# Top-2 gate dispatch on one core: the early two-row store becomes a 64 KB store of zeros, and the first 16 rows are stored whole

## The chip, the cores and the metric

The kernel runs on one core of a Trainium2 chip. The time is the device time of one execution in microseconds (us), and the figure compared is the median of several executions. One core has a vector engine (DVE), a scalar engine (ACT), a general engine (POOL), a tensor engine (PE, not used here) and a synchronisation engine (SP). Sixteen DMA engines move data between the chip's main memory (HBM) and the on-chip memory of 128 partitions. A DMA is issued by one of the engines' instruction queues, written SPq or ACTq in the profile. The DMA transfers issued from SP appear there as queue q1, those from ACT as queue q10.

## What is computed

There are 16 x 1024 = 16,384 tokens. Each has a row x of 512 float32 numbers and 8 router logits. The reference takes a softmax over the 8 logits, keeps the two largest probabilities, smaller one first, scales them so that they sum to one, and writes the row of x twice, once multiplied by each weight:

```python
logits_max = np.max(router_logits, axis=-1, keepdims=True)
probs = np.exp(router_logits - logits_max)
probs = probs / np.sum(probs, axis=-1, keepdims=True)
topk_indices = np.argsort(probs, axis=-1)[..., -k:]          # k = 2
topk_probs = np.take_along_axis(probs, topk_indices, axis=-1)
topk_probs = topk_probs / np.sum(topk_probs, axis=-1, keepdims=True)
x_expanded = x[:, :, np.newaxis, :].repeat(k, axis=2)
return (x_expanded * topk_probs[..., np.newaxis]).astype(np.float32)
```

The inputs are 33.55 MB of x and 0.52 MB of logits; the output is 67.11 MB.

## The kernel before

The 16,384 tokens are laid over 128 partitions, 128 consecutive tokens ("rows") to a partition. So partition p owns 256 KB of x and 512 KB of the output, each in one contiguous piece of HBM. All 128 partitions always move together; "16 rows" below means 16 rows of every partition, 4 MB of x and 8 MB of output.

The **weights** come first. L72 loads all logits with one DMA. `top2_weights` (L26 to L42) finds the largest and second largest logit of every row by a small tournament of maxima and minima on DVE, takes their difference, and ACT turns it into the two weights `WA` by a sigmoid of the difference with each sign (L41, L42).

The **rows** then go in two groups of 64. A group has one input tile `xs` (64 rows a partition) and one extra output tile `osp` (16 rows of doubled output). In each group SP issues four loads of 16 rows (L96), and then DVE walks a plan of seven pieces (L83 to L91). For each piece one DVE multiplication (L99) reads n rows of `xs`, each twice, multiplies them by the two weights and writes 2n rows of output, and one DMA (L107) stores these. A doubled piece needs twice the space of its input, so the output is written over rows of `xs` that are already used up: rows 0 to 15 go to `osp`; rows 16 to 31 go to `low`, the space of rows 0 to 31 of `xs`; rows 32 to 47 go in two halves to `osp` again, after the first 16 rows have been stored from it; rows 48 to 63 go in two halves to `high`, the space of rows 32 to 63.

Two of the seven pieces belong to the first 16 rows: a piece of `e` = 2 rows and one of the other 14. In the first group alone (`rows.start == 0`, L106) the 2-row store is issued from ACT; every other store and every load is issued from SP.

Four things set the order around the change. SP issues strictly in program order: the logits, the four loads of a group, then this group's stores, each of which waits for its multiplication; then the four loads of the next group, which wait until the stores have left `xs`. DVE is in order too, and its third piece of a group (rows 32 to 39) waits until `osp` has been stored. DMAs of one queue are worked off in the order of issue on each of the 16 DMA engines. A DMA of the other queue is interleaved with these. Waits are put in by the framework from the reads and writes of the tiles. At the program's end SP waits for all DMAs (L138).

Of the kernel before, what the change touches and what calls it, by code (L numbers as in the profile page):

```python
# [1 line left out]

# [4 lines left out]

F32 = mybir.dt.float32
ALU = mybir.AluOpType
ACTF = mybir.ActivationFunctionType  # L10
P = 128


def top2_weights(nc, pool, logits, M, E):

    hi, lo, n = None, None, E
    while n > 1:  # L20
        n //= 2
        if hi is None:
            a, b = logits[:, :, 0:n], logits[:, :, n : 2 * n]
            nhi = pool.tile([P, M, n], F32, tag=f"hi{n}")
            nlo = pool.tile([P, M, n], F32, tag=f"lo{n}")
            nc.vector.tensor_tensor(nhi, a, b, op=ALU.max)  # L26
            nc.vector.tensor_tensor(nlo, a, b, op=ALU.min)  # L27
        else:
            a, b = hi[:, :, 0:n], hi[:, :, n : 2 * n]
            nhi = pool.tile([P, M, n], F32, tag=f"hi{n}")  # L30
            nlo = pool.tile([P, M, n], F32, tag=f"lo{n}")
            tmp = pool.tile([P, M, n], F32, tag=f"tmp{n}")
            nc.vector.tensor_tensor(tmp, lo[:, :, 0:n], lo[:, :, n : 2 * n], op=ALU.max)  # L33
            nc.vector.tensor_tensor(nlo, a, b, op=ALU.min)  # L34
            nc.vector.tensor_tensor(nlo, nlo, tmp, op=ALU.max)  # L35
            nc.vector.tensor_tensor(nhi, a, b, op=ALU.max)  # L36
        hi, lo = nhi, nlo
    dlt = pool.tile([P, M], F32, tag="dlt")
    nc.vector.tensor_tensor(dlt, hi[:, :, 0], lo[:, :, 0], op=ALU.subtract)  # L39
    WA = pool.tile([P, M, 2], F32, tag="WA")  # L40
    nc.scalar.activation(WA[:, :, 0], dlt, ACTF.Sigmoid, scale=-1.0)  # L41
    nc.scalar.activation(WA[:, :, 1], dlt, ACTF.Sigmoid, scale=1.0)  # L42
    return WA


@with_exitstack
def kernel(
    ctx: ExitStack,
    tc: tile.TileContext,
    x: bass.AP,  # L50
    router_logits: bass.AP,
    k: bass.AP,
    out: bass.AP,
):
    nc = tc.nc
    B, S, D = x.shape
    E = router_logits.shape[-1]
    N = B * S
    assert int(k) == 2 and E == 8 and N % P == 0
    M = N // P  # L60

    GROUP = 64
    L = 16
    x_v = x.rearrange("b s d -> (b s) d").rearrange("(p m) d -> p m d", p=P)
    o_v = out.rearrange("b s k d -> (b s) k d").rearrange("(p m) k d -> p m k d", p=P)
    rl_v = router_logits.rearrange("b s e -> (b s) e").rearrange(
        "(p m) e -> p m e", p=P
    )

    wpool = ctx.enter_context(tc.tile_pool(name="wpool", bufs=1))  # L70
    logits = wpool.tile([P, M, E], F32)
    nc.sync.dma_start(logits, rl_v)  # L72
    WA = top2_weights(nc, wpool, logits, M, E)

    xs = wpool.tile([P, GROUP, D], F32)
    osp = wpool.tile([P, L, 2, D], F32)


    low = xs[:, : 2 * L, :].rearrange("p (r k) d -> p r k d", k=2)
    high = xs[:, 2 * L :, :].rearrange("p (r k) d -> p r k d", k=2)  # L80
    h = L // 2
    e = 2
    plan = [  # L83
        (0, e, osp[:, :e]),
        (e, L - e, osp[:, e:]),
        (L, L, low),
        (2 * L, h, osp[:, :h]),
        (2 * L + h, h, osp[:, h:]),
        (3 * L, h, high[:, :h]),
        (3 * L + h, h, high[:, h:]),  # L90
    ]  # L91

    for g in range(M // GROUP):
        m0 = g * GROUP
        for r in range(0, GROUP, L):
            nc.sync.dma_start(xs[:, r : r + L, :], x_v[:, m0 + r : m0 + r + L, :])  # L96
        for r, n, og in plan:
            rows = slice(m0 + r, m0 + r + n)
            nc.vector.tensor_tensor(  # L99
                og,  # L100
                xs[:, r : r + n, :].unsqueeze(2).to_broadcast([P, n, 2, D]),
                WA[:, rows, :].unsqueeze(3).to_broadcast([P, n, 2, D]),
                op=ALU.mult,
            )

            queue = nc.scalar if rows.start == 0 else nc.sync  # L106
            queue.dma_start(o_v[:, rows], og)  # L107


# [1 line left out]
_INS = ['x', 'router_logits', 'k']  # L111
_OUTS = [((16, 1024, 2, 512), 'float32')]

_NUMBERS = {'k': 2}


# [26 lines left out]
```

## Time and profile before

| what | value | where it is read |
|---|---|---|
| median of five runs | 241.71 us (241.33 to 241.91) | the times |
| the profiled execution's own time | 241.76 us | the times |
| its span, first to last instruction | 240.0 us | page, first line |
| time outside the span | 1.8 us | difference of the two above |
| DVE busy | 142.1 us (59%) | page, part 1 |
| bytes moved by DMA | 101.19 MB, mean 422 GB/s | page, part 3 |
| one multiplication, 2 / 14 / 16 rows | 2.292 / 15.083 / 17.224 us | groups by form |
| issue of one DMA on SP / ACT | about 0.33 us / 0.376 us | tiles `out_dram`, `osp` |
| 2-row store from ACT: issue, issue to landing | at 16.64 us, 17.3 us | timeline, DMA issues |
| 2-row store from SP (second group): issue, issue to landing | at 134.39 us, 29.8 us | timeline, DMA issues |

The span is cut by the profile into 40 slices of 6 us; for each it gives the busy share of an engine in tenths. Beside this, stretches of any length can be asked for; such a row gives the busy time of each engine, the mean busy share of the 16 DMA engines and the GB/s that they moved. A packet is counted in the stretch in which it starts, so the share of a short stretch can exceed 1. Rate divided by share is then the speed of the DMA engines while they work, free of this effect.

### The profile page before, as it was taken

To read this page: it belongs to the slowest core of one execution; us is meant where nothing else is said; L and a number is where in the kernel's file an instruction comes from. 1 tells how busy PE (TensorE), PEld (TensorE's weight loads), DVE (VectorE), ACT (ScalarE), POOL (GpSimd) and SP (SyncE) were. 2 spreads that over 40 slices of the span, in tenths; PEclk is the share of its full clock that TensorE was granted. 3 is DMA by queue.
4 is the path that set the end of the run, shared out by engine and by line. 5 is a ranking of instruction groups with operands and counts; after the bars stand their busy time and mean duration, and the time that the engine had idled before them with its cause. 6 is when DMAs were issued, how large, how long until landed. Compare 5 with 4: busy or idle time off the path is not lost.

```text
span 240.0 us, 116 instructions
## 1 busy us (share of the span) xinstructions
DVE 142.1 (59%) x25; ACT 1.8 (1%) x3; POOL 0.2 (0%) x4
## 2 busy tenths in 40 slices
DVE  2369999910499999300000999997008999990000
ACT  2000000000000000000000000000000000000000
POOL 0000000000000000000000000000000000000000
DMA  7999999979989899999989999999989898999996
GB/s 262 437 437 389 459 419 426 526 335 440 503 350 524 350 437 437 437 437 437 437 350 437 437 437 437 437 355 531 421 376 503 371 502 355 431 437 437 437 437 262
DMA packets 3312, 101.19 MB, mean 422 GB/s; under 512 B 368, under 2 KB 368, under 8 KB 496
## 3 DMA queue, kind: packets, MB, share of 16 engines
q1 hardware_dynamic: 3168, 100.14, 97.7%
q10 hardware_dynamic: 144, 1.05, 1.0%
HBM read 34.08 MB, written 67.11 MB: 422 GB/s over the span
## 4 chain that ended last, share of the span: by engine, by line
DMA 49%; DVE 32%; issue 7%; SPq 1%; DVEq 0%
DMA out_dram<-osp 26%; DMA xs<-in_x_dram 23%; DVE osp L99 18%; DVE xs L99 15%; SPq L96 0%; SPq L72 0%; SPq L107 0%; DVEq L99 0%
## 5 line engine op out<-in xcount | busy, mean ns | idle before, releaser
L99 DVE TENSOR_TENSOR osp<-xs,WA 128x8192 f32<-128x8192 f32 (+2 forms) x8 | 69.2, 8688 | 69.0 <-DMA xs<-in_x_dram 40.0
L99 DVE TENSOR_TENSOR xs<-xs,WA 128x8192 f32<-128x8192 f32 (+1 forms) x6 | 69.2, 11536 | 0.2
L26 DVE TENSOR_TENSOR nhi<-logits 128x512 f32<-128x512 f32 x1 | 0.7, 691 | 4.5 <-DMA logits<-in_router_logits_dram 4.5
L41 ACT ACT_TABLE_LOAD x1 | 1.3, 1283 | 0.7 <-PEq L124 0.7
L33 DVE TENSOR_TENSOR tmp<-nlo 128x256 f32<-128x256 f32 (+1 forms) x2 | 0.7, 352 | 0.0
L34 DVE TENSOR_TENSOR nlo<-nhi 128x256 f32<-128x256 f32 (+1 forms) x2 | 0.7, 352 | 0.0
L36 DVE TENSOR_TENSOR nhi<-nhi 128x256 f32<-128x256 f32 (+1 forms) x2 | 0.7, 352 | 0.0
L35 DVE TENSOR_TENSOR nlo<-nlo,tmp 128x256 f32<-128x256 f32 (+1 forms) x2 | 0.7, 352 | 0.0
L27 DVE TENSOR_TENSOR nlo<-logits 128x512 f32<-128x512 f32 x1 | 0.7, 684 | 0.0
L41 ACT ACTIVATE WA<-dlt 128x128 f32<-128x128 f32 x1 | 0.3, 314 | 6.3 <-DVE dlt L39 6.3
L39 DVE TENSOR_TENSOR dlt<-nhi,nlo 128x128 f32<-128x128 f32 x1 | 0.3, 292 | 0.0
L42 ACT ACTIVATE WA<-dlt 128x128 f32<-128x128 f32 x1 | 0.3, 298 | 0.0
L124 POOL MEMSET const-bfloat16-1.0<- 128x1 bf16 x1 | 0.1, 101 | 0.0
L124 POOL MEMSET const-uint8-127<- 128x1 uint8 x1 | 0.1, 101 | 0.0
L124 POOL MEMSET const-float32-0.0<- 128x1 f32 x1 | 0.1, 98 | 0.2 <-issue 0.2
L124 POOL MEMSET const-float32-1.0<- 128x1 f32 x1 | 0.1, 98 | 0.0
## 6 DMA issues: line engine op xcount, KB each, us to landing
xs<-in_x_dram SPq DMA_DIRECT2D x8, 4096.0 KB, 36.8
out_dram<-osp SPq DMA_DIRECT2D x4, 4096.0 KB, 20.7
out_dram<-xs SPq DMA_DIRECT2D x4, 4096.0 KB, 22.7
out_dram<-osp SPq DMA_DIRECT2D x2, 7168.0 KB, 31.6
out_dram<-osp ACTq DMA_DIRECT2D x1, 1024.0 KB, 17.3
out_dram<-osp SPq DMA_DIRECT2D x1, 1024.0 KB, 29.8
logits<-in_router_logits_dram SPq DMA_DIRECT2D x1, 512.0 KB, 3.8
out_dram<-xs SPq DMA_DIRECT2D x2, 33.7
```

Of the source, the lines that this page charges most:

```text
L26: nc.vector.tensor_tensor(nhi, a, b, op=ALU.max)
L27: nc.vector.tensor_tensor(nlo, a, b, op=ALU.min)
L33: nc.vector.tensor_tensor(tmp, lo[:, :, 0:n], lo[:, :, n : 2 * n], op=ALU.max)
L34: nc.vector.tensor_tensor(nlo, a, b, op=ALU.min)
L35: nc.vector.tensor_tensor(nlo, nlo, tmp, op=ALU.max)
L36: nc.vector.tensor_tensor(nhi, a, b, op=ALU.max)
L39: nc.vector.tensor_tensor(dlt, hi[:, :, 0], lo[:, :, 0], op=ALU.subtract)
L41: nc.scalar.activation(WA[:, :, 0], dlt, ACTF.Sigmoid, scale=-1.0)
L42: nc.scalar.activation(WA[:, :, 1], dlt, ACTF.Sigmoid, scale=1.0)
L99: nc.vector.tensor_tensor(og, xs[:, r : r + n, :].unsqueeze(2).to_broadcast([P, n, 2, D]), WA[:, rows, :].unsqueeze(3).to_broadcast([P, n, ...
L124: nc = _bacc.Bacc("TRN2", target_bir_lowering=False, num_devices=1)
```

## The change

A tile `blank` of 128 partitions x 128 float32 (64 KB) is set to zero by DVE, and ACT stores it to a scratch tensor `spare` in HBM. Both instructions stand ahead of everything else in the program. The piece of 2 rows and the piece of 14 rows become one piece of 16, in both groups, and all stores of the output are issued from SP.

```diff
     wpool = ctx.enter_context(tc.tile_pool(name="wpool", bufs=1))
+    dpool = ctx.enter_context(
+        tc.tile_pool(name="dpool", bufs=1, space=bass.MemoryType.DRAM)
+    )
+
+
+    blank = wpool.tile([P, 128], F32)
+    spare = dpool.tile([P, 128], F32)
+    nc.vector.memset(blank, 0.0)
+    nc.scalar.dma_start(spare, blank)
+
     logits = wpool.tile([P, M, E], F32)
     nc.sync.dma_start(logits, rl_v)
     WA = top2_weights(nc, wpool, logits, M, E)
...
     h = L // 2
-    e = 2
     plan = [
-        (0, e, osp[:, :e]),
-        (e, L - e, osp[:, e:]),
+        (0, L, osp),
         (L, L, low),
         (2 * L, h, osp[:, :h]),
...
                 op=ALU.mult,
             )
-
-            queue = nc.scalar if rows.start == 0 else nc.sync
-            queue.dma_start(o_v[:, rows], og)
+            nc.sync.dma_start(o_v[:, rows], og)
```

## The prediction

> **What bounds the kernel.** I read the page's busy shares first, then the queue's own waits, then stretches around each change of direction between loads and stores. The page:
>
> ```profile
> span 240.0 us, 116 instructions
> DVE 142.1 (59%) x25; ACT 1.8 (1%) x3; POOL 0.2 (0%) x4
> ...
> DVE  2369999910499999300000999997008999990000
> ...
> DMA  7999999979989899999989999999989898999996
> ...
> HBM read 34.08 MB, written 67.11 MB: 422 GB/s over the span
> ```
>
> DVE has stretches of zeros; the DMA row has none. The chain of waits names DVE for 32% of the span, but while DVE works the DMA engines are full too, so its chain is not what sets the end: the bytes are. 101.19 MB in 240.0 us is 422 GB/s. What DVE and SP wait for costs nothing as long as the DMA engines keep a backlog. The timeline shows how much:
>
> ```profile
> 0.72 0.37 SPq L72 DMA_DIRECT2D logits<-in_router_logits_dram  x1
> 1.15 2.01 SPq L96 DMA_DIRECT2D xs<-in_x_dram  x4
> ...
> 14.31 17.29 DVE L99 TENSOR_TENSOR osp<-xs,WA 128x2048 f32<-128x2048 f32 x2 [6.00 <-DMA xs<-in_x_dram]
> 16.64 0.38 ACTq L107 DMA_DIRECT2D out_dram<-osp  x1
> 31.64 0.35 SPq L107 DMA_DIRECT2D out_dram<-osp  x1
> ```
>
> Four loads and the logits are 17.3 MB; at 433 GB/s (next view) that is 40.0 us from about 1.7 us, so to 41.7 us with nothing else. The 14-row store is queued at 31.64 us, 10 us earlier. The end has a margin too: the last multiplication ends at 215.9 us, the DMA engines work to about 239 us.
>
> So the time changes only if the engines move more bytes, stand idle, or work more slowly. For the last I asked for stretches (length; busy us of DVE, ACT and POOL with counts; clock; DMA share; GB/s):
>
> ```profile
> 18.00:24.00 6.00, 6.00 (x1) 0.00 (x0) 0.00 (x0) 1.00 1.01 389
> 24.00:33.00 9.00, 8.96 (x2) 0.00 (x0) 0.00 (x0) 1.00 1.02 440
> 44.00:46.00 2.00, 2.00 (x1) 0.00 (x0) 0.00 (x0) 1.00 1.68 721
> 118.00:125.00 7.00, 0.00 (x0) 0.00 (x0) 0.00 (x0) 1.00 1.03 393
> 125.00:157.00 32.00, 24.90 (x3) 0.00 (x0) 0.00 (x0) 1.00 1.01 437
> 157.00:160.30 3.30, 3.30 (x1) 0.00 (x0) 0.00 (x0) 1.00 0.95 328
> ```
>
> Rate over share is the engines' speed: 437/1.01 = 433 GB/s in the undisturbed stretch. Time lost in a stretch is share x length less bytes/433. 18 to 24 us: 6.06 - 389 x 6/433 (5.39) = **0.67 us**; this is where the ACT store's packets come among the loads. 118 to 125 us, stores to loads: 7.21 - 6.35 = 0.86. 157 to 160.3 us, loads to stores: 3.14 - 2.50 = **0.64 us**. 44 to 46 us, also loads to stores: 3.36 - 3.33 = **0.03 us**. I have no name for the cause, but four places and their sizes stand in the trace, and the change touches three.
>
> **The change, part by part.**
>
> *Merged multiplications.* In each group 2.292 + 15.083 us become the 16-row form, 17.224 us in its own row. The pair takes 17.29 us in the timeline, so 0.07 us is saved on DVE, worth nothing under the backlog. One L107 issue (0.33 us on SP, in the second group at 134.39) and the ACT issue go; nothing waits for either.
>
> *Whole store, same bytes.* In each group a 1 MB and a 7.3 MB store become one of 8.4 MB. The small packets' own price: 24 to 33 us, where they are interleaved, runs at 440/1.02 = 431, undisturbed 433; 0.4% of 9 us is 0.03 us, twice: **-0.06 us**. The whole store is issued at about 31.6 us, 10 us before the loads are through; should this cover go, each late microsecond costs one. `osp` comes free when it has landed: 17.3 + 0.07 + 8.4 MB = 25.8 MB, the same bytes as before plus 64 KB, so DVE's third piece still starts near 63.3 us, and its store at 72 us stands before the 16-row store behind it has drained (8.4 MB, 19.4 us, to about 81). Cover 9 us. In the second group the store was due at 149.4 us and the loads last to 160: cover 11 us.
>
> *Memset and wait.* The memset is not in the trace. From below by POOL's 128x1 memset (0.098 us), from above by DVE's 128x128 subtraction (0.292 us); I take 0.2. DVE is idle until 4.54 us, so 0. ACT waits for it before issuing; behind that wait stand the table load (1.28 us) and the sigmoids, due at 8.35 us. Some 0.6 us late, the load ends near 2.6: 5.7 us to spare, 0. SP does not wait.
>
> *The scratch store.* Issued near 1 us and 0.38 us long, its first packets come near 2 us, among those of the logits: ahead of the big loads, not of the logits, whose issue begins at 0.72. Everything in the DMA backlog behind it moves. Logits late by 0.9 us would still give weights at 9.8 us, against rows at 14.2. Its price on the engines, lower end: 65.5 KB at 433 GB/s, **0.15 us**. Upper end: the Trainium skill, "DMA: Bandwidth & Descriptors", section Bandwidth, calls transfers under 64 KB dominated by descriptors and measures 0.95 us for 64 KB alone, loaded by another issuing path. By bytes the whole sum is 0.67 us lower than I get below, by the page's figure 0.13 us higher. The nearest row decides: the only other first store of ACT's queue cost 0.67 us of speed at 18 to 24 us. I take 0.15 + 0.67 = **+0.82 us**. No row lets the store bring time directly, and a gain could come only through the stretches below.
>
> *What was paid for the old early store* goes with it: **-0.67 us**.
>
> *First group, loads to stores near 42 us.* Before, 0.03 us, eleven microseconds after the early store's packets. Now nothing has been written to the output by then and no store has run for 38 us. The second group before is the nearest row: pure loads for 37 us, then stores, 0.64 us. From below 0 more (the scratch store readies whatever the early store readied), from above +0.61 by this row, and more if a first touch of the output is dearer. I choose the row: **+0.61 us**. At 118 us nothing changes. At 157 us the first store becomes the whole one; I keep the 0.64, since the one first store of that size in the trace (14 rows, 44 us) is cheap in a place that differs in more than size (second rival).
>
> Sum: 0.82 - 0.67 + 0.61 - 0.06 = **+0.70 us**. The profiled span goes from 240.0 to 240.7 us, its time from 241.76 to 242.46; from the median, 241.71 + 0.70 = **242.4 us** (0.29% slower).
>
> **Rivals.**
>
> *The scratch store does the early store's work.* Then the first-store price only moves from 18 us to 2 us and 42 us stays at 0.03: 0.82 - 0.67 - 0.06 = +0.09, **241.8 us**. The same time comes out if the scratch store costs its bytes alone and only the price at 42 us is new: 0.15 - 0.67 + 0.61 - 0.06 = +0.03. For it: 0.03 us at 44 us against 0.64 at 157. Against: the 64 KB are over near 3 us, and go elsewhere in HBM.
>
> *The 8 KB-a-partition stores are what slows the engines.* This is the other side. Both load-to-store stretches with a loss have the 2-row store as their first store; the one without has the 14-row store. If size decides, both losses end: -0.67 - 0.64 - 0.06 + 0.15 = -1.22, **240.5 us**; with +0.82 for the new small store, -0.55, **241.2 us**. It decides if 42 and 157 us both show some 0.03. Against it: 118 us loses 0.86 us with packets of one size (32 KB) on both sides.
>
> *A first write with no loads beside it is dear.* The ACT store's first packets came late, and loads filled that time. Bare at 42 us, its whole latency would show: issue at 16.64, signs of it from 18 to 24, so up to 2 us beyond my sum: **244.4 us**. Against: loads had no such price at their start.
>
> *The change does not do what it says*: the scratch store might come after the first loads of x. By the issue times it cannot be far behind, and its price is the same there; no separate case.
>
> **How the numbers follow.** Forecast 0.46, first rival 0.26, second 0.21, third 0.07. A measurement of this kernel tells about 0.2%, 0.48 us, from no change. The forecast's spread is 0.4 us either way, so some of it falls under that bound, some of the first rival above it. Slower: 0.36 + 0.07 + 0.07 = 0.50. Same: 0.10 + 0.17 + 0.02 = 0.29. Faster: 0.02 + 0.19 = 0.21. The forecast alone spans 242.0 to 242.8. For 8 in 10 the low end is 240.4, just under all of the second rival; the high end 243.4 leaves out most of the third.
>
> **What would show it.** Right: a stretch near 2 us with a loss near 0.8 us, none at 18 to 24 us, a loss near 0.6 us at 41 to 45 us, and 118 and 157 us as before. If 42 us shows 0.03, the first rival holds; if 157 us also shows none, the second. Any DMA slice below 9 between 31 and 81 us, other than by counting, would mean that a cover I relied on has gone, and the whole sum with it.

## The result and the profile after

The changed kernel takes **242.11 us** (median of 28 runs, 241.72 to 242.76); the kernel before took 241.72 us in 48 runs beside it (241.33 to 242.47). The ratio is **1.0017**, 95% interval 1.0012 to 1.0022: slower by 0.39 us by the medians, 0.29 to 0.53 us by the interval. That is a slowdown clear of zero, though 0.17% is less than the 0.2% (0.48 us) that the prediction counted as just visible.

The page of the changed kernel, with the rows that answer to those of before. Of the last row: the scratch store, its bytes and the time from issue to landing.

```profile
span 240.4 us, 115 instructions
...
DMA  7999999898989899999989999999999998999995
...
HBM read 34.08 MB, written 67.17 MB: 421 GB/s over the span
...
spare<-blank ACTq DMA_DIRECT2D x1, 64.0 KB, 3.7
```

The DMA row still has no gap: its eights stand beside nines, as before, because a packet counts in the slice in which it starts. No stretch of idle DMA engines was opened; the 0.4 us of span must come from bytes or from speed. Now the order of the work, from the timeline of the changed kernel:

```profile
0.73 0.38 SPq L82 DMA_DIRECT2D logits<-in_router_logits_dram  x1
0.82 0.17 DVE L78 MEMSET blank<- 128x128 f32 x1 [0.82 <-PEq L130]
1.02 0.34 ACTq L79 DMA_DIRECT2D spare<-blank  x1
1.16 2.08 SPq L104 DMA_DIRECT2D xs<-in_x_dram  x4
1.39 1.28 ACT L41 ACT_TABLE_LOAD   x1 [1.39 <-DVE blank L78]
...
14.52 17.22 DVE L107 TENSOR_TENSOR osp<-xs,WA 128x16384 f32<-128x16384 f32 x1 [6.19 <-DMA xs<-in_x_dram]
31.77 0.35 SPq L113 DMA_DIRECT2D out_dram<-osp  x1
...
63.65 17.29 DVE L107 TENSOR_TENSOR osp<-xs,WA 128x8192 f32<-128x8192 f32 x2 [14.65 <-DMA out_dram<-osp]
```

The third piece in the kernel before:

```profile
63.30 17.29 DVE L99 TENSOR_TENSOR osp<-xs,WA 128x8192 f32<-128x8192 f32 x2 [14.43 <-DMA out_dram<-osp]
```

The scratch store is issued at 1.02 us, between the logits and the first load of x. The first multiplication starts at 14.52 us (before: 14.31), the third piece at 63.65 (before: 63.30). So 0.21 us of delay is there before the first multiplication, and it grew to 0.35 by 64 us. Three stretches of the DMA engines say where (the last two numbers of a row are DMA share and GB/s). The kernel before, then the changed one:

```profile
18.00:24.00 6.00, 6.00 (x1) 0.00 (x0) 0.00 (x0) 1.00 1.01 389
38.00:47.00 9.00, 9.00 (x1) 0.00 (x0) 0.00 (x0) 1.00 1.05 451
156.00:162.00 6.00, 6.00 (x1) 0.00 (x0) 0.00 (x0) 1.00 0.94 355
```

```profile
18.00:24.00 6.00, 6.00 (x1) 0.00 (x0) 0.00 (x0) 1.00 1.01 437
38.00:47.00 9.00, 9.00 (x1) 0.00 (x0) 0.00 (x0) 1.00 1.10 441
156.00:162.00 6.00, 6.00 (x1) 0.00 (x0) 0.00 (x0) 1.00 1.16 437
```

By the prediction's sum (share x length less bytes/433, good to about 0.07 us in 9 us because the share has two digits) the loss at 18 to 24 us went from 0.67 to 0.00 us. At 38 to 47 us it went from 0.08 to 0.73: that is where the loads run out and the stores begin. At 156 to 162 us, the same switch in the second group, it was 0.72 and is 0.90. One loss vanished and one of about the same size appeared 22 us later, as forecast. Over 18 to 47 us this pair of profiles leaves nothing to explain +0.39 us. Single profiles scatter, so the same stretches were measured in twelve more kernels.

One thing can be read already: which packets are slow. The 38 to 47 us of the changed kernel, cut at 43.1 us (by the packet records of the trace, the first 64 KB packet, which only the whole store has, starts at 43.19 us):

```profile
40.00:43.10 3.10, 3.10 (x1) 0.00 (x0) 0.00 (x0) 1.00 1.01 338
43.10:47.00 3.90, 3.90 (x1) 0.00 (x0) 0.00 (x0) 1.00 1.24 538
```

0.71 us are lost in the first row and none in the second. The last loads before the stores are slow; the packets of the stores run at the undisturbed speed. So it is at the early store of the kernel before: its first packet starts at 20.94 us, and 0.30 of the 0.67 us are lost before it:

```profile
18.00:20.90 2.90, 2.90 (x1) 0.00 (x0) 0.00 (x0) 1.00 0.94 362
```

### The profile page after: what moved, and what is told of

Same layout as the page of the kernel before. It is cut to its first block, busy times and chain, and to the rows that moved or that the text cites. A ratio compares the mean times of both kernels' runs of the same rounds, so it can differ in the third digit from the quotient of the medians.

```text
span 240.4 us, 115 instructions
## 1 busy us (share of the span) xinstructions
DVE 142.1 (59%) x24; ACT 1.8 (1%) x3; POOL 0.2 (0%) x4
## 4 chain that ended last, share of the span: by engine, by line
DMA 46%; DVE 36%; issue 7%; SPq 0%; DVEq 0%
DMA out_dram<-osp 27%; DVE osp L107 22%; DMA xs<-in_x_dram 19%; DVE xs L107 14%; SPq L82 0%; SPq L113 0%; DVEq L107 0%
## 5 line engine op out<-in xcount | busy, mean ns | idle before, releaser
L107 DVE TENSOR_TENSOR osp<-xs,WA 128x8192 f32<-128x8192 f32 (+1 forms) x6 | 69.0, 11534 | 69.4 <-DMA xs<-in_x_dram 39.9
```

What stands on the lines that cost most here:

```text
L107: nc.vector.tensor_tensor(og, xs[:, r : r + n, :].unsqueeze(2).to_broadcast([P, n, 2, D]), WA[:, rows, :].unsqueeze(3).to_broadcast([P, n, ...
```

## The experiments

My theory, as it stood after the result: each first store after a long stretch of loads costs the DMA engines some 0.65 us wherever it stands, and the scratch store costs its bytes. The rivals: the scratch store costs all of it; or the loss of the early store does. Four kernels on one chip took the change apart.

**No scratch store** (`a1_no_scratch`), the changed kernel less these lines and the pool of the scratch tensor:

```diff
-    blank = wpool.tile([P, 128], F32)
-    spare = dpool.tile([P, 128], F32)
-    nc.vector.memset(blank, 0.0)
-    nc.scalar.dma_start(spare, blank)
```

> The changed kernel without its memset and scratch store. Theory (each first store after a long stretch of loads costs the DMA engines about 0.65 us wherever it stands; the scratch store costs its bytes, 0.15 to 0.2 us): no loss at 18 to 24 us, 0.6 to 0.7 us lost near 41 us, and a time 0.15 to 0.2 us under the changed kernel, near 241.9 us. Rival one (the scratch store alone makes the changed kernel slow): 241.7 us, level with the kernel before. Rival two (the scratch store is free, the loss of the early store costs it all): 242.1 us.

**Scratch store added to the kernel before** (`a2_before_plus_scratch`), these lines with their pool and nothing else:

> The kernel before with the memset and the scratch store added, nothing else. Theory: the loss at 18 to 24 us stays at 0.6 to 0.7 us, because a store elsewhere at 2 us readies nothing; time before + 0.15 to 0.2 us, 241.9 us. Rival one: before + 0.4, 242.1 us. Rival two: before, 241.7 us. Rival three (any earlier store readies the way): the loss at 18 to 24 us goes and the time falls to 241.2 us.

**Two pieces, all stores from SP** (`a3_split_all_sp`), the kernel before with one line changed:

```diff
-            queue = nc.scalar if rows.start == 0 else nc.sync
+            queue = nc.sync
```

> The kernel before with its 2-row store of the first group issued from SP, so that it is worked off behind the loads. Theory: no loss at 18 to 24 us, 0.6 to 0.7 us near 41 us, time as the kernel before or up to 0.2 us over it (241.7 to 241.9). If the early store by itself saved time: as the changed kernel without the scratch store.

**Merged in the second group alone** (`a4_whole_second`):

```diff
-        for r, n, og in plan:
+        for r, n, og in plan if g == 0 else [(0, L, osp)] + plan[2:]:
```

> The kernel before with the 2-row and 14-row pieces merged in the second group alone; the early store of the first group stays on ACT. Theory: 0.6 to 0.9 us are still lost at 157 to 160 us, although the first store is now the whole one with 64 KB a partition; time as the kernel before, 241.7 us. Rival (size of the first store decides): 0.03 us lost there, 241.1 us.

Measured, as ratios to the kernel before with 95% intervals:

| kernel | ratio | 18 to 24 us | 38 to 47 us | 156 to 162 us |
|---|---|---|---|---|
| no scratch store | 1.0026 (1.0014 to 1.0037) | 0.00 | 1.06 | 0.50 |
| before plus scratch store | 1.0011 (0.9999 to 1.0023) | 0.37 | 0.08 | 0.77 |
| two pieces, all from SP | 1.0021 (1.0011 to 1.0031) | 0.00 | 1.03 | 0.55 |
| merged in the second group alone | 0.9993 (0.9984 to 1.0002) | 0.57 | 0.08 | 0.72 |

(us lost, worked out as above; where the last packets of the switch start after 162 us the last column misses a little.)

Rival two holds for the most part. Without the scratch store the kernel is no faster than the changed one, and moving the early store from ACT to SP is alone enough for the whole slowdown. The merge in the second group costs nothing, and 0.72 us are still lost there with a first store of 64 KB a partition: the size of the first store does not decide. The scratch store's price lies between nothing and 0.56 us (the upper end of 1.0023); these runs do not fix it better. Two expectations were misses: 241.9 us for the kernel without it, measured 242.2, and at most 241.9 us with all stores from SP, measured 242.3. Beside the scratch store the early store lost 0.37 us, less than the 0.6 to 0.7 expected.

So the early store does something that I had put at 0.06 us. Why does it pay? **First touch** (the first write to a place of the output is dear) was one idea, the **switch of direction** from loads to stores another. Two kernels kept the moment of the early store, cut it to 64 KB, and stored the 16 rows whole:

```diff
-            queue.dma_start(o_v[:, rows], og)
+            if n == e:
+                if g == 0:
+                    nc.scalar.dma_start(o_v[:, 0, 0, :128], osp[:, 0, 0, :128])
+                continue
+            if r == e:
+                nc.sync.dma_start(o_v[:, m0 : m0 + L], osp)
+                continue
+            nc.sync.dma_start(o_v[:, rows], og)
```

This is `b1_touch_out`; `b2_touch_spare` has a scratch tensor `spare` in the place of `o_v[:, 0, 0, :128]`.

> As the kernel before, but the early ACT store carries 64 KB (128 numbers of the first output row of each partition) and the first 16 rows are then stored whole from SP, in both groups; the first 64 KB are written twice with the same numbers. Theory one (the early store saves time because the first write to the output's places costs latency, and loads fill that time when it comes among them): a small touch is enough, some loss at 18 to 24 us, under 0.1 us lost near 42 us, time before + 0.15 us, 241.9 us. Theory two (the switch of all engines from loads to stores costs it, whatever was written earlier): 0.7 to 1.0 us lost near 42 us, 242.2 to 242.4 us.

> As the touch of the output with 64 KB at 16 us, but into a scratch tensor. Theory one (places): 0.7 to 1.0 us lost near 42 us, 242.2 to 242.4 us. Rival (any store among the loads readies the writing): under 0.1 us near 42 us, 241.9 us. Together with the touch of the output this tells places from writing as such, at the same hour and size.

Both lost: ratios 1.0021 (1.0007 to 1.0034) and 1.0015 (1.0005 to 1.0025). The chip of this batch was slower (kernel before: 242.14 us), so only ratios count. The touched output at 18 to 24 and 38 to 47 us:

```profile
18.00:24.00 6.00, 6.00 (x1) 0.00 (x0) 0.00 (x0) 1.00 1.03 442
...
38.00:47.00 9.00, 9.00 (x1) 0.00 (x0) 0.00 (x0) 1.00 1.10 433
```

The packets of the touch cost next to nothing at 18 to 24 us (0.06), and 0.90 us are lost at the switch; with the scratch tensor 0.06 and 1.08. Writing to the output's own places beforehand does not help. The same question was put to the loads, with **the second group loading the first group's rows again** (`b3_loads_again`; half of its output is then computed from other rows):

```diff
-            nc.sync.dma_start(xs[:, r : r + L, :], x_v[:, m0 + r : m0 + r + L, :])
+            nc.sync.dma_start(xs[:, r : r + L, :], x_v[:, r : r + L, :])
```

> The kernel before with the second group loading rows 0 to 63 of x again instead of rows 64 to 127 (half of the output is computed from other rows). Theory one (first touch of places): the loss at 118 to 125 us, 0.86 us before, falls under 0.3 us, and the time by 0.5 us or more to 241.2 us. Theory two (switch of direction): 0.8 us stays, 241.7 us.

1.0007 (0.9992 to 1.0021), and 1.21 us lost at 117 to 131 us, as in the neighbours on that chip (1.25, 1.42 and 1.43; the kernel before on the first chip 0.91). Places read before are no cheaper. First touch has fallen on both sides.

**The early store from ACT in the second group too** (`b5_act_both`), one condition in the kernel before:

```diff
-            queue = nc.scalar if rows.start == 0 else nc.sync
+            queue = nc.scalar if r == 0 else nc.sync
```

> The kernel before with the 2-row store of the second group issued from ACT as well. If an early store saves what the first group shows (some 0.4 us), the same again: a loss of 0.4 to 0.6 us moves from 157 us to about 137 us, 0.03 us stays near 160 us, time 241.3 to 241.5 us. If the first group's gain is a thing of the first write of the program: 241.7 us.

**0.9981** (0.9972 to 0.9990): faster than both kernels. The second 2-row store is issued by ACT at 134.8 us and now goes among the loads of the second group. The stretches 133 to 145 and 156 to 162 us of this kernel:

```profile
133.00:145.00 12.00, 12.00 (x2) 0.00 (x0) 0.00 (x0) 1.00 0.99 418
156.00:162.00 6.00, 6.00 (x1) 0.00 (x0) 0.00 (x0) 1.00 1.00 431
```

0.30 us are lost at the early store and 0.03 at the switch. In time the gain repeats: 0.19% of 242.14 is 0.46 us, so it is not a thing of the program's first write. The trace does not show where it was won. The kernel before, on the first chip, lost 0.01 and 0.72 us in these stretches, 0.40 more in all; but the neighbours on this chip, without an early store in the second group, lost little more than 0.33: 0.45 and 0.34 us in the two touches, and 0.54 in the kernel that loads again, whose rows are:

```profile
133.00:145.00 12.00, 12.00 (x2) 0.00 (x0) 0.00 (x0) 1.00 0.99 429
156.00:162.00 6.00, 6.00 (x1) 0.00 (x0) 0.00 (x0) 1.00 0.88 341
```

That leaves at most some 0.2 us for the switch. Another difference is at the end: by the packet records the 16 engines come to their last packets within 0.55 us of each other here (238.13 to 238.68 us), within 0.92 in the kernel before (237.84 to 238.76) and within 1.24 in the kernel that loads again (237.84 to 239.08). Whether that belongs to the store from ACT was not tested.

What must such a store be: recent, or large? The last four kernels asked.

**A late touch** (`c1_touch_late`), the changed kernel with its 64 KB to a scratch tensor not at the start but when the first multiplication is done, at 31.35 us, from `osp`; no other early store:

```diff
...
+            if rows.start == 0:
+                nc.scalar.dma_start(spare, osp[:, 0, 0, :128])
             nc.sync.dma_start(o_v[:, rows], og)
```

> The whole first 16 rows stored from SP in both groups, and 64 KB stored from ACT to a scratch tensor when the first multiplication is done, near 32 us, some 8 us before the loads run out. Theory recency (a store shortly before the loads run out keeps the way open, whatever its size): under 0.2 us lost at 38 to 46 us, time before + 0.15, 241.9 us if before is at 241.7. Theory volume (it takes a good many store packets among the loads): 0.7 to 1.0 us lost there, time before + 0.4 to 0.5.

**A scratch store of 1 MB at the start** (`c4_scratch_1mb`), in the changed kernel in place of the 64 KB, from `osp` set to zero; no other early store:

```diff
...
+    spare = dpool.tile([P, 2048], F32)
...
+    nc.vector.memset(osp[:, :2], 0.0)
+    nc.scalar.dma_start(spare, osp[:, :2].rearrange("p r k d -> p (r k d)"))
```

> The changed kernel with the scratch store made 1 MB, from zeros in the output tile, near 3 us; 2.4 us of bytes more. Theory recency: 0.7 to 1.0 us lost at 38 to 46 us, since 30 us of pure loads lie between; time before + 2.8 to 3.2 us. Theory volume (a megabyte of stores once, at any hour): under 0.2 us lost there, before + 2.4 to 2.9 us with what it loses near 4 us.

The late touch: 1.0025 (1.0014 to 1.0036). The large scratch store: 1.0090 (1.0069 to 1.0112), 244.2 us beside 241.8. The stretch 38 to 47 us of the late touch, then 4 to 18 and 38 to 47 us of the large scratch store:

```profile
38.00:47.00 9.00, 9.00 (x1) 0.00 (x0) 0.00 (x0) 1.00 1.08 412
```

```profile
4.00:18.00 14.00, 3.73 (x11) 1.19 (x3) 0.00 (x0) 1.00 0.99 412
...
38.00:47.00 9.00, 9.00 (x1) 0.00 (x0) 0.00 (x0) 1.00 1.09 466
```

A small store a few microseconds before the switch leaves 1.16 us of loss. One megabyte in the first 20 us, to places that the output never uses, leaves 0.12, after 0.54 lost at 4 to 18 us (0.12 there in the late touch). The first multiplication had to wait until this store had left `osp` and began at 19.59 us, but the loads lasted to about 44 us and no DMA engine stood idle for it. The added time over the kernel before, 2.4 us, is that of its 1.05 MB at 433 GB/s (2.42). So a megabyte of zeros does what the megabyte of output did; the 64 KB of the change do not.

**One row instead of two** from ACT in both groups (`c2_one_row`, `e = 1` in the fastest version so far) was the middle of the scale:

> The early store from ACT in both groups, with 1 row instead of 2 (0.5 MB). Theory volume: part of the gain is lost, 0.2 to 0.5 us lost at 38 to 46 us, time between the kernel before and 0.45 us under it. Otherwise level with the version with 2 rows from ACT in both groups, 0.45 us under before.

0.9999 (0.9989 to 1.0008), level with the kernel before. Rows of 18 to 24 and 38 to 47 us:

```profile
18.00:24.00 6.00, 6.00 (x1) 0.00 (x0) 0.00 (x0) 1.00 0.95 388
38.00:47.00 9.00, 9.00 (x1) 0.00 (x0) 0.00 (x0) 1.00 1.12 461
```

0.32 and then 0.50 us: half a megabyte takes away about half of the loss at the switch. In this kernel the packets are half as large and as many as with two rows, so volume and packet size are not told apart; only that more of either helps. (The touches too had 128 packets, of 512 bytes each, so the number of packets is not what counts.)

**The mirror image for the loads** (`c3_act_both_load`): the version with both 2-row stores on ACT, and 4 rows of the second group's load issued from ACT as soon as their space is free, among the stores.

```diff
+            f = 4 if g > 0 and r == 0 else 0
+            if f:
+                nc.scalar.dma_start(xs[:, :f, :], x_v[:, m0 : m0 + f, :])
...
```

SP loads the other rows.

> The 2-row store from ACT in both groups, and the first 4 rows of the second group's load (1 MB) issued from ACT as soon as their space is free, near 82 us, so among the stores. If a megabyte of the other direction mixed in works for stores to loads as for loads to stores: the loss at 118 to 125 us falls from 0.9 to 1.3 us to some 0.5 us in all with what shows near 85 to 95 us; time 0.3 to 0.6 us below the version without it, 0.8 to 1.0 us below before. If stores to loads is another thing: no gain, 0.45 us below before.

0.9984 (0.9973 to 0.9995), no better than without it, and it tests less than I meant. As the rows came early, the second 2-row store was issued at 101.52 us, still among stores, and its effect on the switch was lost: 0.42 us at 156 to 162 us again. At 117 to 131 us 0.94 us are lost, as in the neighbours on this chip (0.84 to 0.91). So this kernel gained 0.16% although neither switch of the second group lost less than in the late touch on this chip (0.88 and 0.41): one more sign that the switch alone does not explain the gain in the second group. Whether a mixed megabyte helps from stores to loads is left open.

## Why the prediction was right, and where its terms were off

The mechanism held: DMA engines always busy, no cover lost, the price of a first store moved from 18 us to the switch near 42 us, slower by some tenths. The measured 242.11 us lies inside the range and inside the forecast's own 242.0 to 242.8, below its middle of 242.4. That the number came so near was luck: two terms of the sum were mis-sized, in opposite directions.

*Merged multiplications, whole store, memset and wait* (-0.06 us): harmless, as said. The memset took 0.165 us (I took 0.2), the 16-row multiplication 17.22, the ACT table load ended at 2.7 us, the weights came when they did before, and merging the second group moved the time by nothing that can be told from zero (0.9993). The -0.06 us itself is too small to be seen: 24 to 38 us lost 0.03 us before and 0.02 after, and for the second group, where the small packets stood behind the loads, no row had been read.

*The scratch store* (+0.82 us, of which 0.67 as "the only other first store of ACT's queue"): too dear. The first load of x landed 13.26 us after its issue instead of 13.07, which is 0.19 us. With and without the store, the time differs by 0.11% with an interval from -0.01% to 0.23% in the kernel before; in the changed kernel 1.0017 stands against 1.0026 without it. That agrees with the bytes alone, 0.15 us, and excludes 0.82, but is too coarse to tell 0.15 from twice as much. The Trainium skill's 0.95 us for 64 KB ("DMA: Bandwidth & Descriptors", Bandwidth) was measured on loads issued from GpSimd; for this store among running loads the interval excludes it. Nor did the sign "a loss near 0.8 us near 2 us" come. Before, then after:

```profile
1.60:3.60 2.00, 0.00 (x0) 0.41 (x1) 0.00 (x0) 1.00 0.86 231
```

```profile
1.60:3.60 2.00, 0.00 (x0) 1.07 (x1) 0.00 (x0) 1.00 0.75 205
```

0.65 us were lost there before, 0.55 after; from 4 to 18 us 0.03 and 0.09 (by the packet records the store's own packets start between 3.8 and 4.4 us). So the start of the loads has a loss of its own, which the prediction did not count, and the scratch store added none to it. The step that failed is the choice of the nearest row: what was lost at 18 to 24 us belonged to a megabyte, not to being first. The 64 KB touches of the same queue at the same moment lost 0.06 us.

*The old early store's price* (-0.67) went as forecast: 0.00 at 18 to 24 us.

*The switch near 42 us* (+0.61): too cheap. Over 18 to 24 and 38 to 47 us together, the kernels with 2 rows from ACT in the first group lost 0.75, 0.45, 0.65, 0.78, 0.59 and 0.56 us, mean 0.63; those without lost 0.73 (the changed kernel), 1.06, 1.03, 0.96, 1.14 and 1.16, mean 1.01. The difference is 0.38 us where the prediction had -0.67 + 0.61 = -0.06. The second group's 0.64 us was too low a guide to a bare switch in the first.

Put together, with the scratch store at its bytes: 0.15 + 0.38 = 0.53 us, at the upper end of the measured 0.29 to 0.53. An over-priced scratch store made up for an under-priced switch.

*First rival*: half right in its second form, that the scratch store costs its bytes alone, but its +0.03 us is excluded; its first form is refuted as 64 KB readies nothing. *Second rival* (size of the first store): refuted in the second group, where the first store became one of 64 KB a partition and 0.72 us were lost as before. *Third rival* (a bare first write is dear): its direction is what was found, with 0.38 us in place of up to 2, and it is no matter of first writing. What was said against it, that loads had no such price at their start, was misread: see 1.6 to 3.6 us.

What stays open is the cause inside the DMA engines. Shown is that in the first group the loss at the switch from loads to stores is smaller in all when about a megabyte of stores has gone among the loads, that this holds across some 25 us of pure loads (the large scratch store landed at 19.4 us, the switch came near 44), that it falls on the loads and not on the stores, and that neither the places nor 64 KB shortly before matter. Why the loads slow down when stores are next, and why a new stretch of loads makes the loss due again, is not known. Nor is it shown where the second group's gain was won.

## What to carry to other kernels

When a kernel is bound by bytes, look at the speed of the DMA engines while they are busy (rate over share), stretch by stretch, above all where loads turn to stores. A real store of about a megabyte, issued from the second queue so that it goes among the loads rather than behind them, saved about half a microsecond of kernel time each time here (0.21% in the first group, 0.19% in the second) at no extra bytes; a token of 64 KB saved nothing. Before pricing a new small transfer by the nearest row, ask what that row's price belonged to: its being first, its place, or its volume.

## What was not expected of the hardware

Moving one 1 MB store from ACT to SP in the first group made the kernel 1.0021 times as long; moving one from SP to ACT in the second group made it 0.9981 times as long. The speed of the DMA engines was the same 433 GB/s in every undisturbed stretch; what the queue changes is where the store's packets stand among the loads. The Trainium skill's rule ("DMA: Bandwidth & Descriptors", Rules for kernel authors) is that spreading transfers over issuing queues does not help bandwidth, since all run on the same 16 engines. That agrees with the 433 GB/s, but not with the two ratios: the rule misses an effect of some 0.2% here.
